# Output projections of a two-layer trunk: deeper weight buffers, six modulation steps per tile, and the sum of squares on another engine

## The chip, the cores and the metric

One core of one Trainium2 chip runs the whole kernel in one launch. The metric is the device time in microseconds (us). Three timed executions of the kernel before took 3622.48, 3617.58 and 3610.61 us, a median of 3617.58. Engines are called by their short names in the rows: PE is TensorE, DVE VectorE, ACT ScalarE, POOL GpSimd, SP the queue that issues DMAs.

## What is computed

Two residual layers of one denoising step, over 640 tokens (512 sample, 128 prompt) of 2048 features. Each layer normalizes and modulates its input, runs a mixer, and adds the gated output projection of the mixer's result. The change touches the output projection of both layers, the modulation that the first one computes meanwhile for the second layer, and the last norm:

```python
def rmsnorm(x, g, eps=NORM_EPS):
    xf = x.astype(jnp.float32)
    y = xf * lax.rsqrt(jnp.mean(xf * xf, axis=-1, keepdims=True) + eps)
    return (y * g.astype(jnp.float32)).astype(x.dtype)

def adaln(cond, w, b):
    m = (jax.nn.silu(cond) @ w + b)[:, None, :]
    return jnp.split(m, 3, axis=-1)

    for layer in range(DEPTH):
        ...
        hp = rmsnorm(xp, norm_g[layer]) * (1.0 + scale_p) + shift_p
        ...
        op, new = mixer(hp, layer_params[layer], None, layer)      # ends in  ... @ w_out
        ...
        xp = xp + gate_p * op
        ...
    y_prompt = rmsnorm(xp, final_norm_g)
```

## The kernel before, in words

**Layout.** Features lie on partitions in 16 tiles of 128 (KT = 16), tokens along the free axis (T = 640, in two halves of 320). All products are made in float32 from two parts: an operand is split into hi, rounded, and lo, the rest, and `project_steps` (L111) issues three matmuls for each 128-row step, hi by hi, hi by lo, lo by hi (L126). Weights arrive in parts of 128x512 (256 KB, four steps of the contraction): a DMA (L118) fills `raw`, ScalarE copies it to `whi` (L100), GpSimd subtracts to get `wlo` (L101). `raw` and `whi` have three buffers, `wlo` two. One tile of 128 output features takes four parts, 96 matmuls of 320 columns.

**`out_proj`** (L710) is called twice, in layer 0 (L821) and layer 1 (L1580). Its tile loop (L746 to L759) goes over tiles 0 to 13: project the tile into one of three PSUM buffers; load the residual `xr`; `evac` (L724), two VectorE instructions of 512 and 128 columns that scale the PSUM tile by the gate and add `xr`; seven calls of the modulation generator; then `squares`, where in layer 0 the tile is stored to `x1d` (L729) and ScalarE squares it into `sq` (L730); GpSimd adds `sq` to `acc` (L758); and in layer 0 `premul` (L737) scales the tile on ScalarE once the store has read it. The last two tiles go by halves of the tokens (`half`, L768), so that the statistics of half 0 (`stats`, L773: three matmuls L778, two ScalarE steps L779 and L780 giving `rs`) start before half 1 is projected. At the end `done` is called: in layer 0 `modulate1` (L798 to L819), which multiplies by `rs` on VectorE (GpSimd for every fourth tile of half 1), adds the shift on ScalarE and makes `h1lo` on VectorE; in layer 1 `finish` (L1574), 16 VectorE instructions for each half (L1576) and the output DMAs. The first two tiles of layer 0, and three of layer 1, are `begun` before: three of their four parts are projected while the mixer ends.

**Modulation.** `adaln_steps` (L188) computes four blocks of layer 1's gate modulation during the output projection of layer 0. One call of the generator is one step: a DMA of 256 KB into `araw` (three buffers, two loaded ahead) and two VectorE instructions that add it, weighted, to `aacc` (L198 for a block's first, L200 for the others). After 16 steps and a lag of two calls come TensorE's `ada` (L207), a copy by ScalarE (L210), transposes (L214) and a small add (L155): 19 calls for a block, 76 for the four.

**Order.** Each engine runs its instructions in the order that the scheduler gave them; an instruction that waits holds all that stand behind it on its engine. TensorE reads a tile's last part, then goes on with the next tile in another PSUM buffer, so an evacuation is needed only before the third tile after it starts.

Of the kernel before, what the change touches and what calls it, by code (L numbers as in the profile page):

```python
# [11 lines left out]
F32 = mybir.dt.float32  # L12
# [41 lines left out]
def kernel(  # L54
# [33 lines left out]
    def V(name, i=0, n=1):  # L88
        o = _VEC[name][0] + i
        return vecs[:, o:o + n] if o < NV0 else vec0[:, o - NV0:o - NV0 + n]  # L90
# [12 lines left out]
    def sigmoid(out, in_, tmp, scale=-1.0, bias=None, out_scale=-1.0):  # L103
# [4 lines left out]
        act.activation(out=tmp, in_=tmp, func=AF.Ln, bias=one_b[0:tmp.shape[0]])  # L108
        act.activation(out=out, in_=tmp, func=AF.Exp, scale=out_scale)

    def project_steps(ps, wd, nk, n, xhi, xlo, halves, kc, flip=0, lead=False):  # L111
        order = [c ^ flip for c in range(0, nk, kc)]
        for c in order:
            raw = wp.tile([128, WC], F32, tag="raw", name="raw")
            whi = wp.tile([128, WC], F32R, tag="whi", name="whi")
            wlo = wp.tile([128, WC], F32R, tag="wlo", name="wlo", bufs=2)
            m = kc * n
            dma(out=raw[:, :m].rearrange("p (k n) -> p k n", k=kc), in_=wd[:, c:c + kc, :])  # L118
            split(raw[:, :m], whi[:, :m], wlo[:, :m])
            for g, k in product((0, 1) if lead and c == order[0] else (None,), range(kc)):  # L120
                kk = c + k
                hi, lo = whi[:, k * n:(k + 1) * n], wlo[:, k * n:(k + 1) * n]
                for i, (w, x) in enumerate(((hi, xhi), (hi, xlo), (lo, xhi))):
                    for j, (p, (a, b)) in enumerate(zip(ps, halves)):
                        if g in (None, j):
                            pe.matmul(p[:n, 0:b - a], w, x[:, kk ^ flip, a:b],  # L126
                                      start=(kk == order[0] and i == 0), stop=(kk == order[-1] + kc - 1 and i == 2))
                    yield k == kc - 1 and i == 2
# [56 lines left out]
                pe.transpose(pt[:, j * 128:(j + 1) * 128], row[:, j * 128:(j + 1) * 128], ident)  # L185
            ada_end(layer, n, pt.rearrange("p (j g r) -> p j r g", j=4, g=4)[:, :, 0:2, :], 4)

    def adaln_steps(layer, psp, tag, sb, blocks):  # L188
        for n in blocks:
            acc = adp.tile([128, 2, 512], F32, tag="aacc", name="aacc")  # L190
            ahead = [ada_raw(layer, n, k, sb, 3) for k in range(2)]
            for k in range(KT):
                raw = ahead.pop(0)
                if k + 2 < KT:
                    ahead.append(ada_raw(layer, n, k + 2, sb, 3))
                for s in range(2):
                    if k == 0:
                        dve.tensor_scalar(out=acc[:, s], in0=raw, scalar1=scs[:, k, s:s + 1], scalar2=None, op0=ALU.mult)  # L198
                    else:
                        dve.scalar_tensor_tensor(out=acc[:, s], in0=raw, scalar=scs[:, k, s:s + 1], in1=acc[:, s],  # L200
                                                 op0=ALU.mult, op1=ALU.add)
                yield
            for _ in range(ADA_LAG):
                yield
            ps = psp.tile([128, 512], F32, tag=tag, name="ada")
            for s in range(2):
                pe.matmul(ps[32 * s:32 * s + 32, :], ones[:, 0:32], acc[:, s], start=True, stop=True,  # L207
                          tile_position=(0, 32 * s))
            row = sb.tile([128, T], F32, tag="tmp", name="row")[0:64, 0:512]
            act.activation(out=row, in_=ps[0:64], func=AF.Copy)  # L210
            yield
            pt = psp.tile([128, 512], F32, tag=tag, name="adat")
            for j in range(4):
                pe.transpose(pt[:, j * 64:(j + 1) * 64], row[:, j * 128:(j + 1) * 128], ident[0:64, 0:64])  # L214
            ada_end(layer, n, pt[:, 0:256].rearrange("p (j g r) -> p j g r", j=4, g=2)[:, :, :, 0], 1)
# [500 lines left out]
    def out_proj(layer, yh, yl, wd, acc, sb, psp, dst, x_src, store, flip, done, begun=(), ada=iter(())):  # L716
# [27 lines left out]
            sqs[j] = sb.tile([128, T], F32, tag="tmp", name="sq")  # L744

        for j in range(KT - 2):  # L746
            pt, g = begun[j] if j < len(begun) else out_begin(j, psp[j % len(psp)], wd, yh, yl, flip)
            for _ in g:
                pass
            load(j)  # L750
            evac(j, pt[:, 512 - HT:512 + HT], 0, T)
            for _ in range(7):
                next(ada, None)
            if j:
                square_tile(j)
            squares(j, 0, T)
            if j:
                pool.tensor_tensor(out=acc, in0=acc, in1=sqs[j], op=ALU.add)  # L758
            premul(j, 0, T)  # L759
        last = (KT - 2, KT - 1)  # L760
        for j in last:
# [21 lines left out]
        for i, _ in enumerate(g):  # L783
            if i == 2 * 48 + 11:
                stats(0)
        stats(1)
        done(rs, premul)

    h1hi, h1lo = h0hi, h0lo
# [4 lines left out]
    with tc.tile_pool(name="pso", bufs=1, space=PSUM) as psp, \  # L794
            tc.tile_pool(name="psa", bufs=2, space=PSUM) as psa:
        acc = x1t.tile([128, T], F32, tag="acc", name="acc", bufs=1)
        ada = adaln_steps(1, psa, "psa", x1t, range(NB, 12))

        MORD = ((0, range(10)), (1, range(4)), (0, range(10, 12)), (1, range(4, 8)), (0, range(12, 16)), (1, range(8, 16)))

# [772 lines left out]

    def finish(rs, _):  # L1574
        for (a, b), k in product(HALVES, range(KT)):
            dve.scalar_tensor_tensor(out=x2[:, k, a:b], in0=x2[:, k, a:b], scalar=V("final_g", k), in1=rs[:, a:b],  # L1576
                                     op0=ALU.mult, op1=ALU.mult)
            dma(out=o_y[k][:, a:b], in_=x2[:, k, a:b])

    out_proj(1, y1hi, y1lo, w_o1, acc, x2t, [pj, pj, pj3], x2, x1d, None, 0, finish, begun)  # L1580
# [104 lines left out]
```

## Time and profile before

| | us |
|---|---|
| timed executions | 3610.61, 3617.58, 3622.48 |
| profiled execution | 3616.01 |
| its span | 3614.2 |
| TensorE busy in the span | 3429.2 (95%) |
| VectorE busy | 2121.4 (59%) |
| ScalarE busy | 1564.7 (43%) |
| GpSimd busy | 1217.8 (34%) |
| mean granted TensorE clock | 0.986 of full speed |

Shares are over the whole span. What an edit is worth is read in its own stretch: layer 0's tile loop runs from about 1259.7 to 1462.6 us, its last two tiles and the change to layer 1 up to about 1527 us; layer 1's tile loop from about 3395 to 3565 us, its end up to 3614.2.

### The profile page before, as it was taken

Reading aid. Unit: us, or ns where it says so; the run is one execution under the profiler, and the core shown is the slowest. Engines: PE = TensorE matmul, PEld = TensorE weight load, DVE = VectorE, ACT = ScalarE, POOL = GpSimd, SP = SyncE. Lnnn points to the kernel's source line nnn. Section 1 sums busy time; section 2 is a strip of 40 time slices with the busy share of each in tenths; the row PEclk is TensorE's granted clock in tenths of the full one; section 3 lists DMA queues with packets and bytes.
Section 4 is the critical chain, followed back from the end, with each engine's and each line's share of the span. In section 5 each row is a group of like instructions: output and inputs, shape, how many; then the busy total and the mean of one; then the engine's idle time right before and its main releaser. Section 6 shows DMA issues by size and latency. Waiting matters only on the chain. (4 is left out here: it accounts for less than half of the span.)

```text
span 3614.2 us, 84002 instructions
## 1 busy us (share of the span) xinstructions
PE 3429.2 (95%) x34432; PEld 3004.6 (83%) x34432; DVE 2121.4 (59%) x4218; ACT 1564.7 (43%) x3214; POOL 1217.8 (34%) x1158
## 2 busy tenths in 40 slices
PE   8999999999999989899999999999999999999998
PEld 4788889988898888898887878788888888888898
DVE  3355655666666494536665666666676666666302
ACT  3244443444444422444544534444445445544322
POOL 1322222222232344543333333333333333333444
PEclk9999999999999999999999999999999999999999
DMA  9623433333333365332232222222222222233434
GB/s 324 228 73 99 126 100 111 109 108 108 108 105 107 114 222 166 107 97 66 70 75 60 73 63 69 72 66 68 72 71 70 72 68 72 70 77 104 153 98 143
DMA packets 388610, 376.23 MB, mean 104 GB/s; under 512 B 200512, under 2 KB 242560, under 8 KB 388224
## 3 DMA queue, kind: packets, MB, share of 16 engines
q1 hardware_dynamic: 388224, 370.86, 34.9%
q8 instruction: 270, 4.42, 0.5%
q14 instruction: 116, 0.95, 0.1%
HBM read 328.51 MB, written 42.24 MB: 103 GB/s over the span
## 5 line engine op out<-in xcount | busy, mean ns | idle before, releaser
L101 POOL TENSOR_TENSOR wlo<-raw,whi 128x512 fp32r<-128x512 f32 (+1 forms) x628 | 863.8, 1376 | 1917.9 <-PE pj L126 1207.8
L126 PE MATMUL pj<-h0hi,wlo 128*128 128x320 f32 x4448 | 1087.0, 323 | 25.3 <-POOL wlo L101 25.2
L126 PE MATMUL pj<-h0hi,whi 128*128 128x320 f32 x4448 | 1083.2, 322 | 4.3 <-ACT whi L100 3.1
L126 PE MATMUL pj<-h0lo,whi 128*128 128x320 f32 x4448 | 1077.1, 321 | 2.9 <-DVE h0lo L101 1.6
L126 PEld LDWEIGHTS pj<-h0hi,wlo 128*128 128x128 f32 x4448 | 746.2, 191 | 60.8 <-POOL wlo L101 30.0
L126 PEld LDWEIGHTS pj<-h0hi,whi 128*128 128x128 f32 x4448 | 744.3, 191 | 37.7 <-issue 7.7
L126 PEld LDWEIGHTS pj<-h0lo,whi 128*128 128x128 f32 x4448 | 747.4, 190 | 31.3 <-issue 8.0
L100 ACT ACTIVATE whi<-raw 128x512 fp32r<-128x512 f32 (+1 forms) x628 | 390.8, 623 | 752.5 <-PE pj L126 385.6
L200 DVE SCALAR_TENSOR_TENSOR aacc<-araw,scs,aacc 128x512 f32<-128x512 f32 x480 | 408.5, 900 | 17.4 <-DMA araw<-in_dram 16.3
L364 DVE TENSOR_REDUCE nm<-S 128x1 f32<-128x768 f32 (+1 forms) x120 | 98.5, 820 | 258.3 <-PE S L376 258.3
L1340 ACT ACTIVATE UV<-CC 64x128 f32<-64x128 f32 x160 | 43.2, 270 | 336.6 <-PE CC L1338 307.9
L724 DVE SCALAR_TENSOR_TENSOR x<-pj,mod,xr 128x512 f32<-128x512 f32 (+2 forms) x68 | 33.3, 526 | 250.9 <-PE pj L126 245.3
L367 ACT ACTIVATE P<-S,nm 128x768 f32<-128x768 f32 (+1 forms) x120 | 95.2, 793 | 165.7 <-DVE nm L364 165.0
L1130 DVE TENSOR_TENSOR GG<-gram,con 128x512 f32<-128x512 f32 (+1 forms) x192 | 107.5, 596 | 75.7 <-PE gram L1126 75.4
L1126 PE MATMUL gram<-AR,BK 64*128 64x128 f32 x1280 | 116.6, 296 | 19.3 <-DVE GG L1130 12.3
L1126 PEld LDWEIGHTS gram<-AR,BK 64*128 64x128 f32 x1280 | 92.5, 192 | 44.8 <-DVE GG L1130 23.3
L1062 PE MATMUL plo<-lr,lw 96*128 96x320 f32 x256 | 103.4, 486 | 9.8 <-DMA lr<-lorad 7.3
L566 PE MATMUL po<-PT,vt 128*128 128x128 f32 x800 | 103.2, 276 | 0.1
L566 PEld LDWEIGHTS po<-PT,vt 128*128 128x128 f32 x800 | 98.0, 191 | 4.2 <-issue 2.5
L1354 DVE TENSOR_TENSOR S<-CC,S 128x128 f32<-128x128 f32 (+1 forms) x112 | 29.9, 267 | 119.4 <-PE CC L1305 79.8
L1330 DVE SCALAR_TENSOR_TENSOR rhs<-CC,MV 128x128 f32<-128x128 f32 x160 | 46.2, 289 | 71.1 <-PE CC L1328 70.8
L1338 PEld LDWEIGHTS CC<-rhs,xd 64*64 64x64 f32 x1280 | 50.0, 134 | 41.9 <-DVE rhs L1330 19.5
(340 smaller groups left out, 5164.3 us busy)
## 6 DMA issues: line engine op xcount, KB each, us to landing
raw<-in_dram SPq DMA_DIRECT2D x612, 256.0 KB
araw<-in_dram SPq DMA_DIRECT2D x384, 256.0 KB
lr<-lorad SPq DMA_DIRECT2D x128, 120.0 KB
Ld<-GG SPq DMA_DIRECT2D x64, 160.0 KB
lw<-in_dram SPq DMA_DIRECT2D x128, 48.0 KB
x<-in_dram SPq DMA_DIRECT2D x16, 320.0 KB
xr<-in_dram SPq DMA_DIRECT2D x16, 320.0 KB
DD<-Xd SPq DMA_DIRECT2D x32, 160.0 KB
```

What stands on the lines that cost most here:

```text
L100: act.activation(out=hi, in_=src, func=AF.Copy)
L101: (lo_eng or pool).tensor_tensor(out=lo, in0=src, in1=rf(hi), op=ALU.subtract)
L126: pe.matmul(p[:n, 0:b - a], w, x[:, kk ^ flip, a:b], start=(kk == order[0] and i == 0), stop=(kk == order[-1] + kc - 1 and i == 2))
L200: dve.scalar_tensor_tensor(out=acc[:, s], in0=raw, scalar=scs[:, k, s:s + 1], in1=acc[:, s], op0=ALU.mult, op1=ALU.add)
L364: dve.tensor_reduce(out=nm, in_=S[:, 0:nk], axis=AX.X, op=ALU.max, negate=True)
L367: act.activation(out=P[:, 0:nk], in_=S[:, 0:nk], func=AF.Exp, bias=nm, accum_out=l)
L566: pe.matmul(po[:, 0:128], H.vt[:, kt, :], PT[:, j, :], start=(j == 0), stop=(j == n - 1))
L1062: pe.matmul(ps[:, 0:HT], lw, lo, start=True, stop=True)
L1126: pe.matmul(ps[:, j * 128:(j + 1) * 128], BK[hs, c + j, :, :].rearrange("p a t -> p (a t)"), AR[hs, c + j, :, :].rearrange("p a t -> p (a ...
L1130: dve.tensor_tensor(out=GG[:, c:c + n, h, :], in0=ps[:, 0:n * 128].rearrange("p (j t) -> p j t", t=128), in1=maskg.rearrange("p (o t) -> p ...
L1330: dve.scalar_tensor_tensor(out=rhs.rearrange("p (h d) -> p h d", h=2), in0=C, scalar=-1.0, in1=un.MV[:, s, :].rearrange("p (h d) -> p h d" ...
L1338: pe.matmul(pu[z][o:o + 64, hs], xd[o:o + 64, 2 * loc[z] + h, :], rhs[o:o + 64, hs], start=True, stop=True)
```

## The change

- `project_steps` takes `raw`, `whi` and `wlo` from another pool, with four buffers each, while the list `wide` isn't empty. `out_proj` puts its pool there at tile 4 and takes it out before `done`. This holds for both calls; tiles 0 to 3 keep the buffers of before.
- The generator is called six times a tile from tile 1 on and not at all at tile 0; in this output projection it loads `araw` three ahead, with four buffers.
- The addition of `sq` to `acc` goes from GpSimd to VectorE.
- In `finish` every fourth tile goes by GpSimd (times `rs`) and ScalarE (times the gain) in place of one VectorE instruction.

```diff
+    wide = []
+
     def project_steps(ps, wd, nk, n, xhi, xlo, halves, kc, flip=0, lead=False):
         order = [c ^ flip for c in range(0, nk, kc)]
         for c in order:
-            raw = wp.tile([128, WC], F32, tag="raw", name="raw")
-            whi = wp.tile([128, WC], F32R, tag="whi", name="whi")
-            wlo = wp.tile([128, WC], F32R, tag="wlo", name="wlo", bufs=2)
+            if wide:
+                raw, whi, wlo = (wide[0].tile([128, WC], dt, tag="w" + name, name=name, bufs=4)
+                                 for name, dt in (("raw", F32), ("whi", F32R), ("wlo", F32R)))
+            else:
...
-    def adaln_steps(layer, psp, tag, sb, blocks):
+    def adaln_steps(layer, psp, tag, sb, blocks, ahead_by=2):
...
-            ahead = [ada_raw(layer, n, k, sb, 3) for k in range(2)]
+            ahead = [ada_raw(layer, n, k, sb, ahead_by + 1) for k in range(ahead_by)]
...
         for j in range(KT - 2):
+            if j == 4:
+                wide.append(sb)
...
-            for _ in range(7):
+            for _ in range(6 if j else 0):
                 next(ada, None)
...
-                pool.tensor_tensor(out=acc, in0=acc, in1=sqs[j], op=ALU.add)
+                dve.tensor_tensor(out=acc, in0=acc, in1=sqs[j], op=ALU.add)
...
         stats(1)
+        wide.pop()
         done(rs, premul)
...
-        ada = adaln_steps(1, psa, "psa", x1t, range(NB, 12))
+        ada = adaln_steps(1, psa, "psa", x1t, range(NB, 12), 3)
...
         for (a, b), k in product(HALVES, range(KT)):
-            dve.scalar_tensor_tensor(out=x2[:, k, a:b], in0=x2[:, k, a:b], scalar=V("final_g", k), in1=rs[:, a:b],
-                                     op0=ALU.mult, op1=ALU.mult)
+            if k % 4 == 3:
+                pool.tensor_tensor(out=x2[:, k, a:b], in0=x2[:, k, a:b], in1=rs[:, a:b], op=ALU.mult)
+                act.activation(out=x2[:, k, a:b], in_=x2[:, k, a:b], func=AF.Copy, scale=V("final_g", k))
+            else:
+                dve.scalar_tensor_tensor(out=x2[:, k, a:b], in0=x2[:, k, a:b], scalar=V("final_g", k), in1=rs[:, a:b],
+                                         op0=ALU.mult, op1=ALU.mult)
```

In the rows of the order below a name carries its buffer's number. On GpSimd in layer 0, before, the four parts of tile 5 (`wlo_12803` to `12893`) stand around the addition of tile 4's squares:

```order
L101 TENSOR_TENSOR wlo_12708<-raw_12706,whi_12707 128x512
L101 TENSOR_TENSOR wlo_12738<-raw_12736,whi_12737 128x512
L101 TENSOR_TENSOR wlo_12803<-raw_12801,whi_12802 128x512
L101 TENSOR_TENSOR wlo_12833<-raw_12831,whi_12832 128x512
L758 TENSOR_TENSOR acc_12187<-acc_12187,sq_12794 128x640
L101 TENSOR_TENSOR wlo_12863<-raw_12861,whi_12862 128x512
L101 TENSOR_TENSOR wlo_12893<-raw_12891,whi_12892 128x512
```

The same place after, the last two parts of tile 4 and the four of tile 5 (12765, 12795, 12825, 12855):

```order
L101 TENSOR_TENSOR wlo_12656<-raw_12654,whi_12655 128x512
L101 TENSOR_TENSOR wlo_12686<-raw_12684,whi_12685 128x512
L101 TENSOR_TENSOR wlo_12765<-raw_12763,whi_12764 128x512
L101 TENSOR_TENSOR wlo_12795<-raw_12793,whi_12794 128x512
L101 TENSOR_TENSOR wlo_14662<-raw_14660,whi_14661 128x512
L101 TENSOR_TENSOR wlo_14681<-raw_14679,whi_14680 128x512
L101 TENSOR_TENSOR wlo_12825<-raw_12823,whi_12824 128x512
L101 TENSOR_TENSOR wlo_12855<-raw_12853,whi_12854 128x512
```

The addition has left GpSimd's row of parts, and two parts of layer 1's first projection (14662, 14681) have come into it.

On VectorE the stretch from tile 4's evacuation (`pj_12593`) to tile 5's (`pj_12762`) reads, after:

```order
L730 SCALAR_TENSOR_TENSOR x1_12180<-pj_12593,mod0_88,xr_12714 128x512
L730 SCALAR_TENSOR_TENSOR x1_12180<-pj_12593,mod0_88,xr_12714 128x128
L204 TENSOR_SCALAR aacc_12729<-araw_12730,scs_87 128x512 x2
L206 SCALAR_TENSOR_TENSOR aacc_12729<-araw_12732,scs_87,aacc_12729 128x512
L161 TENSOR_TENSOR mod1_89<-adat_12723,vec0_67 128x8
...
L766 TENSOR_TENSOR acc_12187<-acc_12187,sq_12756 128x640
...
L206 SCALAR_TENSOR_TENSOR aacc_12729<-araw_12895,scs_87,aacc_12729 128x512
L730 SCALAR_TENSOR_TENSOR x1_12180<-pj_12762,mod0_88,xr_12883 128x512
```

Between the two evacuations stand 2 first steps, 19 accumulating instructions (the two rows of L206 shown, 17 left out) and the addition of a tile's squares; between those of tiles 5 and 6 stand 11 and an addition, between those of tiles 6 and 7 only the addition, and these three come again for tiles 7 to 10 and 10 to 13. Before, the evacuations of tiles 5 and 6, and of 8 and 9, have 2 and 19 such instructions between them, the next ones 11, and none of them an addition.

At the end of the kernel, GpSimd's row after has the multiplications of `finish` between the last parts:

```order
L101 TENSOR_TENSOR wlo_41678<-raw_41676,whi_41677 128x512
L1586 TENSOR_TENSOR x2_39919<-x2_39919,rs_41446 128x320 x4
L101 TENSOR_TENSOR wlo_41696<-raw_41694,whi_41695 128x512
L101 TENSOR_TENSOR wlo_41714<-raw_41712,whi_41713 128x512
L101 TENSOR_TENSOR wlo_41732<-raw_41730,whi_41731 128x512
L1586 TENSOR_TENSOR x2_39919<-x2_39919,rs_41446 128x320 x4
```

Before, the four parts stood one behind the other and nothing followed. The three parts behind the first four multiplications are the last three of tile 15's second half.

## Rows read from the trace of the kernel before

**Rows 1.** Windows: span, busy us and count of PE, PEld, DVE, ACT, POOL; PEclk; DMA; GB/s.

```profile
1259.70:1462.60 202.90, 185.10 (x1182) 177.67 (x1183) 131.87 (x158) 52.84 (x91) 91.41 (x61) 0.95 0.59 190
...
1462.60:1527.00 64.40, 51.50 (x301) 47.28 (x300) 43.21 (x86) 38.07 (x86) 35.67 (x26) 0.95 0.34 105
```

**Rows 2.** Groups by form, 1257 to 1465 us: count, busy us, mean ns, idle before.

```profile
L126 PE MATMUL pj<-h0hi,wlo 128*128 128x320 f32 x394 | 95.3, 321 | 16.7 <-POOL wlo L101 16.7
...
L200 DVE SCALAR_TENSOR_TENSOR aacc<-araw,scs,aacc 128x512 f32<-128x512 f32 x120 | 115.8, 1024 | 7.1 <-DMA araw<-in_dram 6.5 <-DVE aacc L200 0.3
...
L101 POOL TENSOR_TENSOR wlo<-raw,whi 128x512 fp32r<-128x512 f32 x51 | 72.7, 1430 | 82.8 <-PE pj L126 51.7 <-ACT whi L100 8.8 <-ACT x L737 7.0
...
L758 POOL TENSOR_TENSOR acc<-acc,sq 128x640 f32<-128x640 f32 x12 | 22.8, 1902 | 30.4 <-ACT sq L730 24.2 <-PE adat L214 6.2
...
L100 ACT ACTIVATE whi<-raw 128x512 fp32r<-128x512 f32 x51 | 31.8, 627 | 90.3 <-PE pj L126 52.1 <-DMA raw<-in_dram 31.1 <-POOL wlo L101 5.0
```

**Rows 3.** Timeline of TensorE in layer 0's tiles: start, us, instruction, idle before.

```profile
1277.27 0.90 PE L126 MATMUL pj<-h0hi,wlo 128*128 128x320 f32 x2 [2.23 <-POOL wlo L101]
...
1324.26 0.90 PE L126 MATMUL pj<-h0hi,wlo 128*128 128x320 f32 x2 [5.33 <-POOL wlo L101]
...
1324.96 0.73 PE L126 MATMUL pj<-h0hi,whi 128*128 128x320 f32 x2
...
1328.82 0.46 PE L126 MATMUL pj<-h0hi,wlo 128*128 128x320 f32 x2
...
1410.44 0.90 PE L126 MATMUL pj<-h0hi,wlo 128*128 128x320 f32 x2 [3.13 <-POOL wlo L101]
```

**Rows 4.** Timeline of all engines before the stall of 1324.26.

```profile
1318.82 1.00 DVE L724 SCALAR_TENSOR_TENSOR x<-pj,mod,xr 128x512 f32<-128x512 f32 x2
...
1319.86 0.74 ACT L730 ACTIVATE sq<-x 128x640 f32<-128x640 f32 x1 [5.02 <-DVE x L724]
...
1320.67 1.86 POOL L758 TENSOR_TENSOR acc<-acc,sq 128x640 f32<-128x640 f32 x1 [7.65 <-ACT sq L730]
...
1322.49 1.71 POOL L101 TENSOR_TENSOR wlo<-raw,whi 128x512 fp32r<-128x512 f32 x1
```

**Rows 5.** Timeline of VectorE: evacuations of tiles 8 to 11 of layer 0.

```profile
1383.88 1.01 DVE L724 SCALAR_TENSOR_TENSOR x<-pj,mod,xr 128x512 f32<-128x512 f32 x2 [13.07 <-PE pj L126]
...
1405.33 1.00 DVE L724 SCALAR_TENSOR_TENSOR x<-pj,mod,xr 128x512 f32<-128x512 f32 x2
...
1418.63 1.01 DVE L724 SCALAR_TENSOR_TENSOR x<-pj,mod,xr 128x512 f32<-128x512 f32 x2 [0.33 <-PE pj L126]
...
1434.46 1.01 DVE L724 SCALAR_TENSOR_TENSOR x<-pj,mod,xr 128x512 f32<-128x512 f32 x2 [13.37 <-PE pj L126]
```

**Rows 6.** Groups by form in layer 1's tile loop, 3395 to 3565 us.

```profile
L126 PE MATMUL pj<-h0hi,wlo 128*128 128x320 f32 x388 | 88.5, 309 | 0.0
...
L758 POOL TENSOR_TENSOR acc<-acc,sq 128x640 f32<-128x640 f32 x12 | 18.9, 1575 | 4.5 <-ACT sq L730 4.5
```

**Rows 7.** Groups by form of TensorE, 1462 to 1530 us.

```profile
L126 PE MATMUL pj<-h0hi,wlo 128*128 128x320 f32 x98 | 30.6, 328 | 6.8 <-POOL wlo L101 6.7
...
L778 PE MATMUL pj<-sq,ones 128*128 128x320 f32 x8 | 3.0, 472 | 2.8 <-ACT sq L730 2.8
```

**Rows 8.** Timeline of VectorE between the layers.

```profile
1484.30 2.92 DVE L809 TENSOR_TENSOR x<-x,rs 128x320 f32<-128x320 f32 x4 [5.85 <-ACT rs L780]
...
1507.42 3.17 DVE L818 SCALAR_TENSOR_TENSOR h0lo<-x,mod,h0hi 128x192 fp32r<-128x192 f32 x8 [1.26 <-ACT h0hi L813]
```

**Rows 9.** Timeline of VectorE at the kernel's end.

```profile
3584.96 8.90 DVE L1576 SCALAR_TENSOR_TENSOR x<-x,vecs,rs 128x320 f32<-128x320 f32 x10 [4.25 <-ACT rs L780]
...
3603.11 7.49 DVE L1576 SCALAR_TENSOR_TENSOR x<-x,vecs,rs 128x320 f32<-128x320 f32 x16 [3.30 <-ACT rs L780]
```

**Rows 10.** Timeline of TensorE at the kernel's end.

```profile
3597.01 0.42 PE L126 MATMUL pj<-h0hi,wlo 128*128 128x320 f32 x1 [0.93 <-POOL wlo L101]
```

**Rows 11.** DMA view, 3603 to 3614 us: the rate in 40 equal slices.

```profile
GB/s 0 0 0 0 0 140 354 321 340 317 326 335 331 340 312 344 321 340 340 307 331 321 354 298 363 151 233 331 349 289 354 312 363 312 358 79 0 0 0 0
```

More of the change, by code (lines that the diff above doesn't have):

```diff
@@ L113, in project_steps @@
         for c in order:
-            raw = wp.tile([128, WC], F32, tag="raw", name="raw")
-            whi = wp.tile([128, WC], F32R, tag="whi", name="whi")
-            wlo = wp.tile([128, WC], F32R, tag="wlo", name="wlo", bufs=2)
+            if wide:
+                raw, whi, wlo = (wide[0].tile([128, WC], dt, tag="w" + name, name=name, bufs=4)
+                                 for name, dt in (("raw", F32), ("whi", F32R), ("wlo", F32R)))
+            else:
+                raw = wp.tile([128, WC], F32, tag="raw", name="raw")
+                whi = wp.tile([128, WC], F32R, tag="whi", name="whi")
+                wlo = wp.tile([128, WC], F32R, tag="wlo", name="wlo", bufs=2)
             m = kc * n
@@ L186, in adaln @@
             ada_end(layer, n, pt.rearrange("p (j g r) -> p j r g", j=4, g=4)[:, :, 0:2, :], 4)
-    def adaln_steps(layer, psp, tag, sb, blocks):
+    def adaln_steps(layer, psp, tag, sb, blocks, ahead_by=2):
         for n in blocks:
             acc = adp.tile([128, 2, 512], F32, tag="aacc", name="aacc")
-            ahead = [ada_raw(layer, n, k, sb, 3) for k in range(2)]
+            ahead = [ada_raw(layer, n, k, sb, ahead_by + 1) for k in range(ahead_by)]
             for k in range(KT):
                 raw = ahead.pop(0)
-                if k + 2 < KT:
-                    ahead.append(ada_raw(layer, n, k + 2, sb, 3))
+                if k + ahead_by < KT:
+                    ahead.append(ada_raw(layer, n, k + ahead_by, sb, ahead_by + 1))
                 for s in range(2):
```

## Prediction

> **What bounds the kernel now.** I read the page first: TensorE is busy 95% of the span, so a gain must come from the stretches where it isn't. The view of windows then goes stage by stage. In layer 0's tile loop TensorE has 185.1 us of work in 202.9, at a granted clock of 0.95 of full speed, 2.4 GHz for most of it and 1.2 behind the stalls; the two half tiles with the change to layer 1 have 51.5 in 64.4 [rows 1]. Layer 1's tile loop is another matter: there the rows have no idle time at all and 309 ns a matmul [rows 6], so buffers or a lighter GpSimd can give nothing in it.
>
> How much layer 0's loop loses is read from its evacuations. An undisturbed tile takes 14.08 us (13.07 idle and 1.01 of the evacuation before it at 1383.88), and 15.83 when a modulation block's products lie in it (1418.63 to 1434.46) [rows 5]. Tiles 2 to 13 need 12 x 14.08 + 4 x 1.75 = 176.0 us; they get 202.9 [rows 1]. So 26.9 us are lost: 16.7 as TensorE waiting for `wlo` [rows 2], the rest mostly as clock, since after a stall a pair of matmuls takes 0.73 us instead of 0.46 for some microseconds [rows 3].
>
> Why `wlo` is late is read from the timeline before the worst stall. VectorE adds modulation steps and reaches tile 4's evacuation only at 1318.82; ScalarE, which had waited 5.02 us for it, squares it at 1319.86, GpSimd, idle for 7.65, adds the squares from 1320.67 for 1.86 us, and the next tile's `wlo`, which stands behind that addition, begins at 1322.49 [rows 4]. TensorE waits 5.33 us [rows 3]. The other large stalls (2.23 and 3.13 there, and one of 4.49 like them) follow late evacuations in the same way: tile 9's comes 21.45 us after tile 8's (1383.88 to 1405.33) where TensorE took 15.83, so 5.6 late [rows 5]. VectorE is late because seven steps of two instructions at 1.024 us [rows 2] and an evacuation of 1.0 don't fit into 14.08. The evacuation itself isn't wanted so early, PSUM having three buffers; what hurts is GpSimd waiting for it with only two `wlo` ahead.
>
> **The addition on VectorE, six steps, deeper buffers (layer 0's loop).** GpSimd's wait goes: its row holds parts only. What is late next is ScalarE. There the square of a tile stands behind the next tile's four copies and ahead of the first copy of the tile after it. With four buffers the next tile is split by then, so a late evacuation reaches TensorE only if it comes more than 14.08 + 0.3 (the hi products that run before the first lo) - 1.0 (evacuation) - 0.74 (square) - 0.63 (copy) - 1.43 (`wlo`) = 10.6 us late [rows 2, 4, 5].
>
> How late will it be? Steps still come in bunches: 2 first steps and 19 others before tile 5's evacuation, as many as before tile 9's in the old kernel, which was 5.6 late from a clean start [rows 5]. The addition comes on top. The trace doesn't show it on VectorE: it lies between 1.0 (the evacuation's two instructions over the same 640 columns, 1.00 [rows 4]) and 1.9 (GpSimd's [rows 2]); I take 1.1, since 1.024 is the mean of one VectorE instruction of 512 columns there. That makes 6.7 late. Tile 6 has 11 x 1.024 + 1.1 + 1.0 = 13.4, under 14.08; tile 7 has the addition alone and is on time again. So 6.7 against 10.6: about 4 us in hand, and VectorE's 12 additions (13 us) lie beside TensorE. If that cover is gone, each excess comes three times (tiles 5, 8, 11).
>
> Tiles 2 and 3 keep the old buffers. Tile 2 now has 16 + 2 steps ahead of its evacuation and is about 5 us late, and its square stands on ScalarE ahead of the third part of tile 3: evacuation, square, copy and `wlo` take 3.8, so the part is ready about 9 us after TensorE went on, and wanted after two parts of 3.52 and the 0.3: a stall of 1.9, more or less. The stall of 2.23 at 1277.27 [rows 3] lies in this early part, whose two `wlo` stay; transfers of the third `araw` ahead of weights add perhaps 1 to 2, and the clock behind these stalls 2. I leave 8 us of the 26.9 in place, bounds 3 (half of the listed stalls gone) and 14 (both stalls as large as the old ones). **Layer 0's loop: -19**, from -24 to -13.
>
> **Half tiles and change to layer 1.** TensorE waits 6.8 us for `wlo` and 2.8 for a square here [rows 7]. The weights are now four ahead, and two parts of layer 1's first projection have been split in tile 5. But from `rs` at 1484.30 VectorE works almost without a break (its only real gap there is 1.26, at 1507.42) [rows 8], so what counts is how much earlier `rs` comes and how much less GpSimd stands beside it. Of 9.6 us idle I take a bit under half: **-4.5**; zero if VectorE's chain is all, -9 if all goes.
>
> **Layer 1.** Its loop has no stall to remove. Its start takes new buffers at tile 4 and I see about 1 us in hand there: **0**, up to +2. At the end TensorE has three waits for split weights, 2.6 us in sum (the last 0.93 [rows 10]), and VectorE's multiplications between the last evacuations are slowed by GpSimd, 0.89 us each (8.90 for 10) against 0.468 (7.49 for 16) when alone [rows 9]; I take 3 us for both. The last half of `finish` changes: 12 on VectorE and 4 on GpSimd. GpSimd's price isn't in the trace for 320 columns; half of 1.575 [rows 6] is 0.79. If the two run beside each other, 12 x 0.468 = 5.6 us, 1.9 less than now; if they exclude each other, 5.6 + 3.2 = 8.8, 1.3 more. The gain can't be had, since the 16 outputs of 160 KB, 2.6 MB at about 330 GB/s [rows 11], take 7.9 us anyway; I take +1.0. In the first half GpSimd's four stand ahead of tile 15's last three `wlo`, about 3 us, while TensorE does tile 14's second half, 14.08 / 2 = 7 us: hidden. **End: -2**, from -4 to +1.5.
>
> The rule of the Trainium skill that speaks against both moves is in "SBUF — State Buffer", section "Who interferes with whom": a VectorE instruction with two SBUF inputs and a GpSimd instruction reading SBUF share a port, and the second waits for the whole of the first. Rows agree in direction: GpSimd's addition takes 1.902 us beside VectorE's steps [rows 2] and 1.575 in layer 1 [rows 6]. By it alone the last half of `finish` would be 8.8 and the sum 0.3 worse.
>
> **Sum.** -19 - 4.5 + 0 - 2 = -25.5 against the profiled execution's 3616.0 (span 3614.2 and 1.8 around it), so 3590.5. The median of the three runs, 3617.58, is 1.6 above that execution: **3592**. The bounds add up to -37 and -9.5: 3580 to 3608.
>
> **Rivals.**
> *The first tiles' stalls go as well* (0.17). The 8 us left in place are my least founded term: fewer additions on GpSimd and none of the seven-step bunches in tile 0 could clear them, with more of the change to layer 1. -26 - 9 - 2 = -37: 3580. Against it: those tiles have the old buffers.
> *Late evacuations reach TensorE through ScalarE* (0.10). It decides from a lateness of 10.6. Tiles 5 and 6 hold 30 steps; 3.9 us in hand are 0.13 us a step, so from a mean of about 1.15 us it bites. At 1.2: 30 x 0.05 = 1.5 and the DMAs' waits 1 us, 2.6 each for three bunches and 1.5 of clock behind each, 12: 3604. For it: the additions make VectorE's bunches longer, and VectorE and GpSimd slow each other. Against: 1.024 was measured with GpSimd's additions running. The skill's port rule, taken at its word, would put whole `wlo` into VectorE's way here and so give this case; the measured 1.024 says that only part of it happens.
> *VectorE becomes the bound* (0.05, the slower side). Three tiles take 44.0 us of TensorE (3 x 14.08 + 1.75) and hold 32 steps, three evacuations and three additions (6.3) and about 1.6 of waits: 36.1 us for 32 steps, 1.13 each. Beyond that every 0.1 us costs 3.2 us per three tiles; the 25 us are used up at about 1.39. At 1.45 it takes 3 x 10.2 = 31 and half-speed stretches of 7: 3630. For it: single steps as long stand in the trace where GpSimd works and transfers are late. Against: a mean so far over 1.024 with GpSimd relieved.
> *It gives nothing* (0.06): the stalls are put down to `wlo` but their real cause is the raw weights' transfer, or the deeper buffers take transfers earlier and collide with `araw`. 3617. Against it: the chain of the 5.33 stall, which shows no transfer.
>
> **How the numbers follow.** The forecast has 0.62, its own range 3584 to 3600. About 0.3% (11 us) is what a measurement of this kernel can tell from no change, so faster means under 3606.7: the forecast, the first rival and a little over half of the second, 0.85; slower is the VectorE case, 0.05; the rest 0.10. The range from 3577 to 3606 takes in the forecast's bounds, most of the first rival and half of the second.
>
> **What would show it.** In layer 0's loop: evacuations of tiles 5, 8 and 11 some 6 to 7 us after TensorE ended the tile, and no wait of TensorE behind them; evacuations of tiles 4, 7, 10 and 13 on time; three tiles in 44 us; granted clock near 1.0 after tile 4; GpSimd without waits for `sq`. `rs` of layer 0 some 21 us earlier. In layer 1's loop no change. At the end the last `rs` about 3 us earlier against TensorE's loop, the outputs ending about 9 us behind it. I am wrong if `wlo` still stops TensorE in tiles 5 to 13 (then it was transfers), if VectorE's steps go over 1.13 us, or if the half tiles lose what the loop gained because VectorE's chain to layer 1 is as long as before.

## The result and the profile after

The changed kernel takes 3586.9 us (median of four executions, 3582.78 to 3592.59) against 3614.97 (four, 3610.61 to 3622.48): a ratio of 0.9927, with an interval of 0.9902 to 0.9951. The forecast was 3592. Its profiled execution spans 3586.1 us, 28.1 less than before. A second set on one chip gave 0.993 (0.9909 to 0.9952); one of its six executions of the changed kernel took 12555.87 us and is left out of that ratio, and nothing here shows why it took so long.

Two executions of one kernel differ by several microseconds in stretches that the change doesn't touch, so the gain is read stage by stage. For that the same TensorE instructions are looked up in two traces and their start times subtracted. Up to the start of layer 0's tile loop the changed kernel is 3.5 us late; between the change to layer 1 and layer 1's output projection it wanders by 6 us and comes back. The kernel before has one kept profile, and so has each edited kernel further down; three profiles that share the changed kernel's loop give it -20.9, -19.3 and -19.9, so a loop is read to within 1 or 2 us. In the stretches that the change touches:

| stretch | forecast | measured |
|---|---|---|
| layer 0's tile loop, all four modulation products | -19 | -20.9 |
| half tiles and change to layer 1 | -4.5 | -8.0 |
| layer 1's loop | 0 | 0.0 |
| layer 1's half tiles and end | -2 | -2.7 |

The windows of the changed kernel, read as [rows 1] (the first is the loop, the second the half tiles up to `rs`, the third VectorE's stretch from `rs` to its last `h1lo`):

```profile
1263.25:1445.20 181.95, 179.02 (x1181) 173.34 (x1181) 142.84 (x171) 55.03 (x96) 80.29 (x53) 0.98 0.68 224
1445.20:1466.50 21.30, 21.30 (x143) 20.67 (x142) 2.01 (x5) 9.73 (x18) 11.40 (x10) 1.00 0.50 158
1466.50:1507.30 40.80, 35.55 (x212) 33.36 (x211) 40.14 (x81) 26.06 (x64) 14.55 (x11) 0.92 0.11 35
```

The loop takes 181.95 us where it took 202.8, at a granted clock of 0.98 instead of 0.95. All waits of TensorE in it, in the timeline (start, length, instruction, idle before), are now two, both in tile 2; there were seven, three of which stand in [rows 3]:

```profile
1263.25 0.56 PE L132 MATMUL pj<-h0hi,wlo 128*128 128x320 f32 x2 [0.73 <-POOL wlo L101]
...
1276.10 0.90 PE L132 MATMUL pj<-h0hi,whi 128*128 128x320 f32 x2 [2.61 <-ACT whi L100]
...
1277.85 0.90 PE L132 MATMUL pj<-h0hi,wlo 128*128 128x320 f32 x2 [0.32 <-POOL wlo L101]
```

(The first row is the loop's start.) VectorE's evacuations, where [rows 5] stood:

```profile
1283.27 1.01 DVE L730 SCALAR_TENSOR_TENSOR x<-pj,mod,xr 128x512 f32<-128x512 f32 x2 [2.94 <-PE pj L132]
...
1311.43 1.01 DVE L730 SCALAR_TENSOR_TENSOR x<-pj,mod,xr 128x512 f32<-128x512 f32 x2 [10.54 <-PE pj L132]
...
1333.50 1.00 DVE L730 SCALAR_TENSOR_TENSOR x<-pj,mod,xr 128x512 f32<-128x512 f32 x2
...
1346.60 1.00 DVE L730 SCALAR_TENSOR_TENSOR x<-pj,mod,xr 128x512 f32<-128x512 f32 x2
...
1355.45 1.01 DVE L730 SCALAR_TENSOR_TENSOR x<-pj,mod,xr 128x512 f32<-128x512 f32 x2 [6.22 <-PE pj L132]
...
1376.51 0.99 DVE L730 SCALAR_TENSOR_TENSOR x<-pj,mod,xr 128x512 f32<-128x512 f32 x2
```

The first row is tile 2, the second tile 4; both are on time (VectorE idle until TensorE ends). TensorE ends tile 5 15.83 later, at 1327.26, so its evacuation at 1333.50 is 6.2 late; tile 6's is 5.3 late, tile 7's on time again, tile 8's 5.2 late. No wait of TensorE follows, and from tile 5 to tile 13 (1311.40 to 1443.40) its granted clock is 1.00. Groups, as [rows 2]:

```profile
L206 DVE SCALAR_TENSOR_TENSOR aacc<-araw,scs,aacc 128x512 f32<-128x512 f32 x120 | 111.6, 994 | 0.4 <-DMA araw<-in_dram 0.4
L132 PE MATMUL pj<-h0hi,wlo 128*128 128x320 f32 x386 | 89.9, 313 | 1.0 <-POOL wlo L101 1.0
...
L101 POOL TENSOR_TENSOR wlo<-raw,whi 128x512 fp32r<-128x512 f32 x54 | 81.6, 1524 | 102.7 <-ACT whi L100 82.8 <-PE pj L132 12.4 <-DMA araw<-in_dram 3.3
...
L766 DVE TENSOR_TENSOR acc<-acc,sq 128x640 f32<-128x640 f32 x13 | 12.2, 942 | 3.2 <-ACT sq L736 3.2
```

An accumulating instruction, two of which make a step, takes 994 ns, an addition on VectorE 942, and the wait for `wlo` has gone from 16.7 to 1.0 us (0.72 and 0.73 of them stand at the loop's start). At the end of the kernel, where [rows 9] stood:

```profile
3558.33 10.42 DVE L1589 SCALAR_TENSOR_TENSOR x<-x,vecs,rs 128x320 f32<-128x320 f32 x10 [3.89 <-ACT rs L788]
3568.68 0.66 DVE L730 SCALAR_TENSOR_TENSOR x<-pj,mod,xr 128x192 f32<-128x192 f32 x2
...
3570.19 0.66 DVE L730 SCALAR_TENSOR_TENSOR x<-pj,mod,xr 128x192 f32<-128x192 f32 x2
3573.31 8.15 DVE L1589 SCALAR_TENSOR_TENSOR x<-x,vecs,rs 128x320 f32<-128x320 f32 x12 [2.46 <-ACT rs L788]
```

```profile
3558.38 4.13 POOL L1586 TENSOR_TENSOR x<-x,rs 128x320 f32<-128x320 f32 x4 [0.84 <-ACT rs L788]
3562.48 4.54 POOL L101 TENSOR_TENSOR wlo<-raw,whi 128x512 fp32r<-128x512 f32 x3
3573.35 4.06 POOL L1586 TENSOR_TENSOR x<-x,rs 128x320 f32<-128x320 f32 x4 [6.33 <-ACT rs L788]
```

The last half of `finish` takes 8.15 us for 12 instructions on VectorE, where it took 7.49 for 16, and GpSimd's four take 4.06, 1.0 each.

### The profile page after: what moved, and what is told of

It reads as the page before. It is cut to its first block, busy times and chain, and to the rows that moved or that the text cites. A ratio compares the mean times of both kernels' runs of the same rounds, so it can differ in the third digit from the quotient of the medians.

```text
span 3586.1 us, 83883 instructions
## 1 busy us (share of the span) xinstructions
PE 3419.8 (95%) x34432; PEld 2999.3 (84%) x34432; DVE 2139.9 (60%) x4236; ACT 1569.4 (44%) x3222; POOL 1180.4 (33%) x1140
## 5 line engine op out<-in xcount | busy, mean ns | idle before, releaser
L206 DVE SCALAR_TENSOR_TENSOR aacc<-araw,scs,aacc 128x512 f32<-128x512 f32 x480 | 404.6, 892 | 9.5 <-DMA araw<-in_dram 8.9
```

## Experiments: each edit alone

The forecast took the loop's gain to be the path of the squares, and with that the three edits to be parts of one thing. The first runs make one edit in the kernel before, or leave one out. Their loops are given as differences to the kernel before, like the table's; the expectations of the later runs still quote rougher readings of the first four (200.7, -2, +2, +11 and -20 for 200.0, -2.8, +2.9, +11.5 and -20.3).

The addition alone:

```diff
-                pool.tensor_tensor(out=acc, in0=acc, in1=sqs[j], op=ALU.add)
+                dve.tensor_tensor(out=acc, in0=acc, in1=sqs[j], op=ALU.add)
```

> The kernel before with one edit: the addition of squares goes from GpSimd to VectorE. Layer 0's tile loop took 202.8 us before and 180.2 after. Theory (a late evacuation reaches TensorE only through what stands behind it in an engine's order): GpSimd's row is free, what is left is ScalarE's order, which lets an evacuation be about 10.6 us late. With seven steps a tile the bunches of VectorE follow each other more closely: tile 4 about 4 late, tile 5 about 5, tile 6 about 12, so one stall of some 2 us with its clock behind it, and the early ones. Loop 184 to 190. Rival 1 (GpSimd's addition is the only cause): loop 180 to 182. Rival 2 (the shallow buffers are the cause): 198 to 203.

Measured: 3615.29 us, loop -2.8, change to layer 1 +2.2. None of the three ranges holds it. The groups of its loop (TensorE; count, busy, mean, idle before and its cause):

```profile
L126 PE MATMUL pj<-h0hi,wlo 128*128 128x320 f32 x406 | 95.8, 315 | 2.3 <-POOL wlo L101 2.3
...
L207 PE MATMUL ada<-aacc,ones 128*32 128x512 f32 x16 | 8.0, 841 | 12.0 <-DVE aacc L200 12.0
```

The wait for `wlo` fell from 16.7 [rows 2] to 2.3 us, as the theory had it. But the modulation's product (L207) now waits 12.0 us for VectorE's sum, where it waited 1.7 before: of 14.4 us, 10.3 have come back there. The three waits in the timeline:

```profile
1301.67 1.00 PE L207 MATMUL ada<-aacc,ones 128*32 128x512 f32 x1 [3.99 <-DVE aacc L200]
```
```profile
1339.85 2.48 PE L207 MATMUL ada<-aacc,ones 128*32 128x512 f32 x4 [4.89 <-DVE aacc L200]
```
```profile
1420.02 1.88 PE L207 MATMUL ada<-aacc,ones 128*32 128x512 f32 x4 [3.08 <-DVE aacc L200]
```

The deeper buffers alone, that is, `wide` as in the diff of the change and nothing else of it:

> The kernel before with one edit: four buffers for each weight part from tile 4. Theory: GpSimd's addition now stands behind all four parts of the next tile instead of two, so an evacuation may be 14.4 - 1.0 - 0.74 - 1.86 - 1.43 = 9.3 us late; tile 4 (7.3 late) costs nothing any more, tile 6 comes about 12 late and costs some 3 us with clock. Loop 185 to 191, so this edit alone gives most of the gain as well, and the two are not to be added up. Rival 1 (the addition on GpSimd must go): 200 to 203. Rival 2 (buffers are the cause): 180 to 183. The change to layer 1 gains as in the changed kernel if the early split of layer 1's first parts is what gave it: 6 us over the stretch from the end of the loop to the second projection's steady run.

Measured: 3612.34 us, loop +2.9, change to layer 1 -6.2, end -5.1. The loop (205.7) refutes the theory's 185 to 191 here too, and lies in neither rival's range; TensorE waits for the same product, for instance

```profile
1424.16 2.48 PE L213 MATMUL ada<-aacc,ones 128*32 128x512 f32 x4 [5.87 <-DVE aacc L206]
```

Six steps alone, three ahead:

> The kernel before with one edit: six modulation steps a tile from the second, loaded three ahead. Theory: bunches of 2 first steps and 21 others come three times with a clean start, each 6 to 7 us late, and the addition still stands on GpSimd behind two parts of the next tile: three or four stalls of 4 to 5 us with their clock. Loop 197 to 206, no gain to speak of. Rival (VectorE's load is what counts): 180 to 190.

Measured: 3627.81 us, loop +11.5. That is a loop of 214, beyond the range, though its cause is the theory's: three waits for `wlo`, one for each bunch, all of this size, and none for the product (a wait of 5.07 for a copy in tile 2, of the kind that is 2.61 in the changed kernel, comes on top):

```profile
1348.73 0.90 PE L126 MATMUL pj<-h0hi,wlo 128*128 128x320 f32 x2 [6.88 <-POOL wlo L101]
```

So each edit alone gives nothing or costs: -2.8, +2.9, +11.5. The changed kernel without the deeper buffers:

```diff
             if j == 4:
-                wide.append(sb)
+                pass
...
-        wide.pop()
```

> The changed kernel without the deeper buffers: addition on VectorE, six steps, and the change at the end remain. Theory: VectorE's lateness stays at 5 to 6 us at tiles 5, 6, 8, 9, 11, 12, and ScalarE's order allows about 10, as the square still stands behind the next tile's four copies: loop 180 to 184, so in the loop the deeper buffers aren't needed. The change to layer 1 loses its gain of 6 us, if that came from splitting layer 1's first parts early. Total 3588 to 3595. Rival (buffers are the cause): loop 195 to 203.

Measured: 3602.14 us, loop -20.3, change to layer 1 +2.0, end +2.8. The loop is as theory had it, and the whole of its gain is there without the deeper buffers. The total is above the expected 3588 to 3595: the change to layer 1 loses not 6 but 10 us of its gain, and the end 5.5. A new theory had to explain why the addition alone gives 2.8 and the addition with six steps 20.3.

## Experiments: the place of the modulation's product

In TensorE's order of the kernel before the four products stand inside tile 3, near its end (`pj_12486`, behind 83 of its 96 matmuls), and behind tiles 5, 8 and 10. With the addition moved it is the same, but for four matmuls in tile 3. The first:

```order
L126 MATMUL pj_12486<-h0lo_96,whi_12578 128x320 x2
L126 MATMUL pj_12486<-h0hi_95,wlo_12579 128x320
L207 MATMUL ada_12456<-aacc_12222,ones_73 32x512 x2
L126 MATMUL pj_12486<-h0hi_95,wlo_12579 128x320
L126 MATMUL pj_12486<-h0hi_95,whi_12578 128x320 x2
```

In the changed kernel the first stands between tiles 4 and 5 (the others between 7 and 8, 10 and 11, 13 and 14):

```order
L132 MATMUL pj_12593<-h0lo_96,whi_12685 128x320 x2
L132 MATMUL pj_12593<-h0hi_95,wlo_12686 128x320 x2
L213 MATMUL ada_12718<-aacc_12260,ones_73 32x512 x2
L132 MATMUL pj_12762<-h0hi_95,whi_12764 128x320 x2
L132 MATMUL pj_12762<-h0lo_96,whi_12764 128x320 x2
```

What differs is VectorE's work while TensorE does the tile ahead of the product. In the changed kernel VectorE, once it has evacuated tile 3, has no steps left of that block, only the addition, and is on time at tile 4. With seven steps it still adds: in the run with the addition moved TensorE ends tile 5 at 1334.95 and wants the product, while VectorE has twelve instructions of the block behind its evacuation of tile 4, six of them from 1334.29 on. Of the four products only the one behind tile 8 doesn't wait, and there VectorE has no steps left behind its evacuation of tile 7:

```profile
1326.92 1.00 DVE L724 SCALAR_TENSOR_TENSOR x<-pj,mod,xr 128x512 f32<-128x512 f32 x2
...
1334.29 6.08 DVE L200 SCALAR_TENSOR_TENSOR aacc<-araw,scs,aacc 128x512 f32<-128x512 f32 x6 [0.56 <-DMA araw<-in_dram]
...
1376.49 1.00 DVE L724 SCALAR_TENSOR_TENSOR x<-pj,mod,xr 128x512 f32<-128x512 f32 x2
...
1387.05 1.01 DVE L724 SCALAR_TENSOR_TENSOR x<-pj,mod,xr 128x512 f32<-128x512 f32 x2 [7.46 <-PE pj L126]
```

(The rows are the evacuation of tile 4, the block's last instructions, and the evacuations of tiles 7 and 8.) The kernel before hid this: its stalls for `wlo` held TensorE back until the sum was there. Two runs test it. First, the changed kernel with seven steps, two ahead:

```diff
-            for _ in range(6 if j else 0):
+            for _ in range(7):
...
-        ada = adaln_steps(1, psa, "psa", x1t, range(NB, 12), 3)
+        ada = adaln_steps(1, psa, "psa", x1t, range(NB, 12), 2)
```

> The changed kernel with seven steps a tile, two loaded ahead, as before; addition on VectorE and deeper buffers remain. New theory: the modulation's products stand in the middle of tiles 3, 6 and 9 again and TensorE waits there for VectorE, 3 to 6 us each with its clock: loop 196 to 205, nearly all of the loop's gain gone, and the change to layer 1 still 6 us shorter. Rival (my first theory: the squares' path alone decides): loop 183 to 189.

Measured: 3618.67 us, loop +0.7 (203.6), change to layer 1 -6.2. The waits, of 1.86, 6.37 and 3.78 us, are for the product, in tile 3 and behind tiles 5 and 10 (its expectation has them in the middle of tiles 3, 6 and 9), and one of 3.22 is for what follows it:

```profile
1342.21 2.48 PE L213 MATMUL ada<-aacc,ones 128*32 128x512 f32 x4 [6.37 <-DVE aacc L206]
...
1350.11 0.69 PE L220 MATMUL adat<-con,row 64*128 64x64 f32 x4 [3.22 <-ACT row L216]
```

Second, seven steps and old buffers, the addition on VectorE, and the product moved by a longer lag between a block's last step and its product (the later blocks' steps come three calls later for each block with it):

```diff
-    def adaln_steps(layer, psp, tag, sb, blocks):
+    def adaln_steps(layer, psp, tag, sb, blocks, lag=ADA_LAG):
...
-            for _ in range(ADA_LAG):
+            for _ in range(lag):
...
-        ada = adaln_steps(1, psa, "psa", x1t, range(NB, 12))
+        ada = adaln_steps(1, psa, "psa", x1t, range(NB, 12), 5)
```

> The kernel before with two edits: the addition of squares on VectorE, and in this output projection a lag of five calls instead of two between a modulation block's last step and its product. Seven steps a tile and the old buffers remain. The lag moves only the place of the product: it now stands at the boundary of tiles 3 and 4, 6 and 7, 9 and 10, 12 and 13, behind a tile with no steps on VectorE. With the addition alone the loop took 200.7 us. New theory (the product's place is what six steps bring): loop 181 to 187, no wait of TensorE for the modulation sum. Rival (the smaller number of steps a tile, or loading three ahead, is what counts): loop 195 to 201.

Measured: 3604.25 us, loop -19.9 (183.0), where the addition alone gave -2.8. The waits for the product are down from 12.0 to 3.7 us, all of it at the first block, whose product now stands behind tile 3, while VectorE has ten instructions of the block behind its evacuation of tile 2:

```profile
L126 PE MATMUL pj<-h0hi,wlo 128*128 128x320 f32 x402 | 93.5, 311 | 1.7 <-POOL wlo L101 1.7
...
L207 PE MATMUL ada<-aacc,ones 128*32 128x512 f32 x16 | 5.7, 709 | 3.7 <-DVE aacc L200 3.7
```

This settles what six steps bring: not less work for VectorE, which has the same 64 steps, but the product at a place where VectorE has none left of that block.

The other half of the theory was that the squares' path can be freed by either of the two other edits. The changed kernel with the addition back on GpSimd:

> The changed kernel with the addition of squares back on GpSimd; six steps and deeper buffers remain. New theory, from the first four runs (each edit alone gave -2, +2 and +11 us in layer 0's loop, six steps with the addition on VectorE -20): with seven steps the modulation's product stands on TensorE in the middle of a tile, where VectorE is late with the sum it reads, so a stall removed behind late squares comes back there (3.99, 4.89 and 3.08 us in the run with the addition moved). Six steps put it behind a tile in which VectorE has no steps. Then either of the other two edits frees the squares. Here the addition stands behind four parts, which allows 9.3 us of lateness, and the tiles come 6 to 7 late: loop 180 to 184, change to layer 1 again 6 us shorter. Rival (the addition on GpSimd must go in any case): loop over 195.

Measured: 3592.82 us, loop -15.6, change to layer 1 -7.7. Neither range: 187.2 against 180 to 184 and over 195. The deeper buffers do most, but against the three profiles of the changed loop 3.7 to 5.3 us are given up: 1.12, 0.23 and 0.76 us of waits for `wlo` in the three bunches, and 2.9 us more of waits in the first tiles, which one profile can't put down to the addition. The timeline shows why an evacuation 6.9 us late costs something where 9.3 were worked out:

```profile
1333.98 1.00 DVE L730 SCALAR_TENSOR_TENSOR x<-pj,mod,xr 128x512 f32<-128x512 f32 x2
1334.90 4.72 DVE L206 SCALAR_TENSOR_TENSOR aacc<-araw,scs,aacc 128x512 f32<-128x512 f32 x7
```
```profile
1335.90 5.15 POOL L766 TENSOR_TENSOR acc<-acc,sq 128x640 f32<-128x640 f32 x1 [7.02 <-ACT sq L736]
1341.01 6.02 POOL L101 TENSOR_TENSOR wlo<-raw,whi 128x512 fp32r<-128x512 f32 x4
```

GpSimd's addition takes 5.15 us, not 1.86 [rows 4], while VectorE's accumulating instructions beside it take 0.67 each (4.72 for 7) and are not slowed at all; the same happens in the two other bunches (5.15 us each). The Trainium skill says in "SBUF — State Buffer", section "Who interferes with whom", that of two such instructions the one that comes second is blocked; the trace agrees in part: here GpSimd, which began at 1335.90 during one of them, stands not for that one alone but until VectorE pauses, at 1339.62. Elsewhere in this loop it is VectorE that comes second: an accumulating instruction that began during an addition took 2.05 to 2.08 us, and the addition 1.6 to 2.0. GpSimd's mean for 13 additions is 2.474 us (a mean of 1.575 in layer 1 [rows 6]). So taking the addition off GpSimd also takes these long additions out of the path; no run shows their share of the 3.7 to 5.3 us.

## Experiments: the rest

Where the change to layer 1 gains is read from the runs above: with the deeper buffers it is -8.0, -7.7, -6.2 and -6.2, without them +2.2, +0.5, +2.0 and +3.5. How, the windows show. VectorE's stretch from `rs` to its last `h1lo` is as long as ever, 40.80 us; before and in the run without the deeper buffers it took

```profile
1484.30:1525.50 41.20, 29.44 (x161) 26.51 (x160) 39.89 (x80) 27.15 (x66) 19.96 (x14) 0.92 0.25 72
```
```profile
1468.70:1509.90 41.20, 27.73 (x154) 24.68 (x153) 41.03 (x80) 27.27 (x66) 20.47 (x14) 0.91 0.25 72
```

The difference stands in TensorE's count: 212 matmuls within VectorE's 40.8 us, against 161 and 154. From the last `h1lo` to layer 1's first `plo` product it is 36.9 us in seven profiles with the deeper buffers (38.7 with them from the first tile) and 44.1 to 46.4 in the five without. Weights that are already split let it do the first products of layer 1 while VectorE makes `h1lo`, so less is left when VectorE ends. That fewer conflicts with GpSimd or an earlier `rs` would do it, as the forecast had it, isn't seen: from the loop's end to `rs` the stretch took 21.7 us before and 21.3 now.

The edit to `finish` was left out of the changed kernel, with the changed kernel beside it on the same chip:

```diff
-            if k % 4 == 3:
-                pool.tensor_tensor(out=x2[:, k, a:b], in0=x2[:, k, a:b], in1=rs[:, a:b], op=ALU.mult)
-                act.activation(out=x2[:, k, a:b], in_=x2[:, k, a:b], func=AF.Copy, scale=V("final_g", k))
-            else:
-                dve.scalar_tensor_tensor(...)
+            dve.scalar_tensor_tensor(...)
```

> The changed kernel as it is, on the same chip as the next two, for their comparison: 3583 to 3593 us.

Measured: 3597.65, 3589.66, 3586.76, 3605.41 and 3581.29 us; by stages, loop -19.3, change to layer 1 -8.0, end -2.6.

> The changed kernel without the edit to finish: all 16 multiplications of each half on VectorE again. From layer 1's loop to the end of the span the changed kernel gained 2.7 us against the kernel before, as did the other runs with this edit and the deeper buffers (2.6 and 2.7), while the run with the deeper buffers alone gained 5.1. So the edit costs about 2.4 us: profile 2 to 3 us shorter from layer 1's loop to the end, and a time of about 3584.5, within the scatter of the runs. If the edit helps as my prediction's first half had it (VectorE relieved beside GpSimd), the end is 1 to 2 us longer instead.

Measured: 3586.85 us, median of six from 3578.09 to 3595.89; ratio to the kernel before 0.992 (0.9905 to 0.9936). That can't be told from the changed kernel's 0.993 by the times. In the profiles the end is told apart: -5.0 us from layer 1's loop to the end of the span against -2.6 and -2.7 in the two profiles of the changed kernel. The edit costs 2.4 us. VectorE, as above:

```profile
3550.89 7.86 DVE L1585 SCALAR_TENSOR_TENSOR x<-x,vecs,rs 128x320 f32<-128x320 f32 x10 [3.89 <-ACT rs L788]
3558.67 0.67 DVE L730 SCALAR_TENSOR_TENSOR x<-pj,mod,xr 128x192 f32<-128x192 f32 x2
...
3562.15 0.68 DVE L730 SCALAR_TENSOR_TENSOR x<-pj,mod,xr 128x192 f32<-128x192 f32 x2
3565.29 7.49 DVE L1585 SCALAR_TENSOR_TENSOR x<-x,vecs,rs 128x320 f32<-128x320 f32 x16 [2.46 <-ACT rs L788]
```

In the first half ten instructions take 7.86 us where they took 10.42 beside GpSimd's, so tile 14's evacuation comes 3.5 us ahead of tile 15's instead of 1.5. Then `rs` is 0.6 us earlier against layer 1's loop, the last half takes 7.49 again instead of 8.15, and the span ends 3.5 us behind it instead of 4.7. The other -5.1 at this end are the deeper buffers' alone (-5.1 with them as the one edit; +2.8 with `finish` edited and the old buffers, where GpSimd's multiplications stand ahead of `wlo` with no reserve).

Two more tries were made at the early wait, which is in tile 2 (the expectations call it tile 3). Deeper buffers from the first tile:

```diff
-            if j == 4:
+            if j == 0:
```

> The changed kernel with the deeper buffers from the first tile of each output projection instead of the fifth. In the changed kernel the loop still loses 2.61 and 0.32 us of waiting and the clock behind it in tile 3, the last that is fed by the old buffers. If the old buffers are the cause: loop 176 to 179, against 180.2. If the early tiles lose to transfers of the modulation's weights: 179 to 184. Layer 1's start may gain or lose 1 us.

Measured: 3594.03 us. TensorE has no wait in the tiles any more, but one of 9.79 us ahead of them, for the copy of tile 0's last weight part, which goes into a new buffer:

```profile
1247.70 12.76 SPq L124 DMA_DIRECT2D raw<-in_dram  x3
```
```profile
1263.72 0.63 ACT L100 ACTIVATE whi<-raw 128x512 fp32r<-128x512 f32 x1 [5.23 <-DMA raw<-in_dram]
```
```profile
1264.41 0.90 PE L132 MATMUL pj<-h0hi,whi 128*128 128x320 f32 x2 [9.79 <-ACT whi L100]
```

The part's transfer is the third of the queue's row, issued at 1260.13 after a wait of 5.5 us for GpSimd's last `h0lo` of the mixer. In the changed kernel the queue has the same wait of 5.5 us, but ahead of `xr`, with the last parts of tiles 0 and 1 already issued. From before TensorE's wait to the loop's end this run gains about 15.6 us, 5 less than the changed kernel, and neither expected range (176 to 179, 179 to 184) is met. A shorter window around the tiles alone would have shown a gain of 27.

Modulation weights two ahead, with `finish` as before:

> The changed kernel without the edit to finish, and with the modulation's weights loaded two ahead as in the kernel before. In the changed kernel TensorE waits 2.61 us in tile 3 for a copy whose raw weights were issued behind eight transfers of modulation weights; two ahead puts five there. Loop to the same point 2 to 4 us shorter than the changed kernel's (the wait and its clock), if that transfer is the cause; no shorter, if the old buffers of tiles 2 and 3 are. With finish as before 2.4 us more: about 3581 in all, at most 3589.

Measured: 3587.94 us (3578.49 to 3596.42), loop -16.1. The wait for the copy in tile 2 fell to 1.14, from 2.61 in the changed kernel and 2.38 in the run without the edit to `finish`, which differs from this one in the loading alone; five transfers of `araw` stand ahead of the part's now, and seven there (the expectation has eight), the last of them issued only when VectorE's steps had freed a buffer (1270.65). So the transfer's place bears on it, but a new wait came behind the first product:

```profile
1317.92 0.68 PE L220 MATMUL adat<-con,row 64*128 64x64 f32 x4 [5.90 <-ACT row L216]
```

The two other runs with the deeper buffers and two ahead have such a wait too (4.16 and 3.22). So 4 to 5 us are lost where 2 to 4 were to be gained, and nothing is better than the changed kernel without the edit to `finish`.

## Why the prediction was right, step by step

- **What bounds.** The stretches and the chain (late evacuation, square, GpSimd's addition, `wlo`) were right: with the addition moved alone, the wait for `wlo` falls from 16.7 to 2.3 us.
- **Loop, -19 against -20.9.** The lateness of 6.7 us (6.2, 5.2 and 5.4 at tiles 5, 8 and 11) and its harmlessness, the addition's 1.1 us (0.94), and three tiles in 44 us (1311.43 to 1355.45 are 44.02) are right. The 8 us left in the first tiles were 6, which is luck: the stall of 1.9 in tile 3 behind a late evacuation of tile 2 did not come (that evacuation was on time, at 1283.27). What stayed were 2.61 and 0.32 us of waits in tile 2 with their clock, the larger for a part whose transfer stands behind seven of `araw`; the forecast had such transfers at 1 to 2 us.
- **What was missing there.** The forecast took six steps as a matter of VectorE's load, and its sum has no term for TensorE waiting for VectorE's modulation sum; the 1.7 us of that wait in the loop before don't appear in it. It is what the other two edits run into: without six steps they give nothing together (+0.7), where the same reasoning gave 183 to 189 us (203.6 measured). It also counted the deeper buffers as part of the loop's cover, and the loop gains 20.3 without them. That the forecast came out is luck in this part: the change has all the edits, and the order of the changed kernel, from which lateness was read, has the product in its good place.
- **Change to layer 1, -4.5 against -8.0.** Inside the bounds, for another reason. The term was built on an earlier `rs` and less of GpSimd beside VectorE; VectorE's stretch is 40.8 us to 41.2 as before. What gave was TensorE's earlier work under it.
- **End, -2 against -2.7.** Two sizes were off and cancel in part: the deeper buffers give 5.1, not 3, and the edit to `finish` costs 2.4, not 1.0. GpSimd's price was taken as 0.79 from half of a longer instruction and is 1.0; the slower first half (10.42 us) was taken for hidden.
- **Rivals.** From tile 5 on lateness reached TensorE through ScalarE in neither profile of the changed kernel, and the mean of an accumulating instruction on VectorE stayed under 1.0 us (0.994 and 0.976). That more of the first tiles' stalls go was not seen; two of them stayed.

## What to carry to other kernels

When a stall is removed, look at every other wait of the engine that it held back, also those that are small now: one that the stall covered can take its place, here 10.3 of 14.4 us. An instruction of the bottleneck engine that reads a slow engine's sum belongs behind a stretch in which that engine has a pause, and a lag of a few calls did that here as well as fewer calls (-19.9 and -20.3). Edits that give -2.8 and +11.5 us alone gave -20.3 together, so leave-one-out runs tell more than single edits; and compare stage by stage between the same instructions, from ahead of the first wait, where executions scatter by more than an edit is worth.

## What the runs showed of the hardware

A GpSimd addition of two SBUF operands (128x640) that took 1.575 us with VectorE mostly idle took 5.15 us beside a row of seven of VectorE's accumulating instructions, which ran at 0.67 us each: GpSimd was held back until VectorE paused, and VectorE was not held. This came three times in 13 additions of one run. In the other direction, in the same run, an accumulating instruction that began during an addition took 2.05 to 2.08 us; and VectorE's multiplications at the end took 1.04 us each (10.42 for 10) beside four GpSimd multiplications and three `wlo`, and 0.468 without GpSimd. Executions of the changed kernel differed by up to 24 us within one set (3581.29 to 3605.41). Part of such scatter lies where nothing was changed: between the layers, with the same order on TensorE, the edited kernels stood -8.4 to +3.9 us against the one profile of the kernel before.
